# Feed-forward products in another order: sums of weights by accumulating DMA, left forms made at their first use, pool roles exchanged, and other prices in the planner

## The chip, the cores and the metric

The kernel runs on one core of a Trainium2 chip. A core has a matrix engine (TensorE, PE in the profile), a vector engine (VectorE, DVE), an activation engine (ScalarE, ACT), a general engine (GpSimd, POOL), a sequencer that mostly starts DMAs (SyncE, SP), and 16 DMA engines that move data between HBM and the on-chip memory SBUF. Matmul results go to PSUM, which has eight banks of 128 x 512 fp32. Each engine runs its instructions in program order; semaphores tie the engines together. The metric is the device time of one execution, in microseconds; lower is better.

## What is computed

A model of four layers on 512 tokens of width 1024, all in fp32. Each layer is a mixer (another one in each layer: RWKV-7, sliding-window attention, a spatial gating unit, gated linear attention) and a SwiGLU feed-forward network (FFN) of hidden width 2816:

```python
def swiglu(x, w_in, w_out):
    gate, up = jnp.split(x @ w_in, 2, axis=-1)
    return (jax.nn.silu(gate) * up) @ w_out
...
    for i in range(DEPTH):
        t, j = i % N_MIXERS, i // N_MIXERS
        hn = rmsnorm(h, norm_mix[i])
...
        h = h + m
        h = h + swiglu(rmsnorm(h, norm_ffn[i]), ffn_w_in[i], ffn_w_out[i])
    return rmsnorm(h, norm_final)
```

The change touches the FFN and what feeds it. The mixers compute the same as before, in code that isn't touched.

## The kernel before

**A product in three matmuls.** Every fp32 operand is split into a high half in a reduced fp32 format and a low half, the rest: ACT copies the high half (`whi`), DVE subtracts to get the low half (`wlo`; both in `split`). `mm3` then adds up high x high, high x low and low x high in the same PSUM bank.

**Seven products instead of eight.** Each FFN matrix is cut into 2 x 2 quarters, and a 2 x 2 block product is done with seven quarter products m1 to m7 (Strassen's way, in a form whose sums chain). `seven` (L764) writes them down: it loads one quarter of weights at a time into `wraw` tiles (`load`, two DMAs of 512 KB on SP's queue for a quarter of 512 x 512), forms sums of weights in place, and multiplies by "left forms", that is quarters of the activations and their sums: x11, x12 and x22 are quarters; s5 = x22 - x21, and s6, s7, s3 follow from it (`combine`, L649). A sum of weights is made either by an accumulating DMA that POOL issues, which adds another quarter from HBM into a `wraw` tile (`add`), or by a DVE addition of two tiles. With p, s and r for three pairs of PSUM banks, and with the weight quarters 0 to 3 of which a, e, b and c are loaded from 0, 1, 2 and 3, the order is:

```
m1: p  = x11 * a            (a = W0)
m2: s  = x12 * e            (e = W1)
m5: r  = s5  * b            (b = W2, + W0 by accumulating DMA)
m6: p += s6  * b            (b += c, on DVE)
m3: r += s3  * c            (c = W3)
m7: p += s7  * c            (c += W2, by accumulating DMA)
m4: p += x22 * b            (b += W1, by accumulating DMA)
```

A product of a full quarter is 24 matmuls: four blocks of the inner dimension, two output banks, three matmuls each. The generator yields after each product, and its caller empties the banks.

**Where it runs.** `ffn` (L722) goes through three parts of the hidden width. Each part has two `hidden` blocks (L828, gate and up projections, SiLU, product, transposition) and one `out_fast` (L751, down projection, added into the residual `h`). Four of the six hidden blocks have quarters 512 columns wide (weights `ffn_w_a`), two 384 (`ffn_w_b`); the output weights are `ffn_o_a` and `ffn_o_b`. The first two products of the next hidden block are written ahead of each output block. In `hidden`, ACT copies m1, m5, m6 and m7 out of PSUM (`copy`) into tiles that wait for their partners; `give` multiplies gate and up and transposes them into the quarters of the output product. In the last output block of a layer, `finish` (L593) follows when a quarter of `h` is complete: it takes the squares for the norm, transposes the quarter and scales it into quarters of the next product.

**Left forms.** Those of the hidden blocks are made once for an FFN, in `quarter` (L640), called by `finish` as soon as the data is there. They stay for all six blocks. Those of an output product are made when `seven` asks for them, through `left_of` (L747). `operand` (L709) hands the left forms to the FFN.

**Pools.** `wraw` has 8 buffers (`wr`), `whi` and `wlo` four each; PSUM tiles (`ps`) 8; general 128 x 512 tiles come from `slot()` (L509, 45 buffers, "slot") or from `more()` (L513, 15 buffers, "left").

**What sets the order on the engines.** The code above only records operations. Class `Program` (L190) then plans all of them: at each step `run` takes the operation that could start first by its prices, within a window of 700 operations, and writes it to its engine. `price` (L262) holds the estimated nanoseconds of an operation; `record` (L225) notes the size of a DMA in `columns`, which `run` turns into a transfer time. Where the planner foresees that PE would idle, `keep_warm` (L391) inserts fill products (L453, 128 x 128 by the identity, result unused) to keep PE's clock up. So whatever is recorded is issued from line 233, and names of tiles, not lines, tell the work apart. Nothing of the plan is fixed on the chip but the order within an engine.

## Time and profile before

| | |
|---|---|
| time, median of 3 runs | 2758.0 us (2755.4 to 2764.08) |
| the profiled execution | 2758.16 us, of which the span of the profile is 2756.5 us |
| mean granted PE clock in it | 0.981 of full speed |
| read from HBM, written | 324.90 MB, 2.10 MB |
| the four FFNs in the span | 556 to 937, 1108 to 1488, 1768 to 2131, 2373 to 2745 us |

A row of a view by groups gives the engine, the operation, output tile <- input tiles, shapes and count, then busy time and mean nanoseconds of one, then the idle time just before. A row of a timeline gives start, length, engine and what ran; brackets hold idle time before it and what ended that. "[0.2 <-DVE wlo L233]" says that the engine sat idle for 0.2 us until a `wlo` was written by DVE. Fills count as busy PE, so a high busy share of PE alone does not say that its time is used.

### The profile page before, as it was taken

How to read it: one execution, taken by the hardware profiler on the slowest of the kernel's cores; microseconds unless marked ns; L12 is line 12 of the kernel's file. 1: busy time of each engine (PE TensorE's matmuls, PEld its weight loads, DVE VectorE, ACT ScalarE, POOL GpSimd, SP SyncE). 2: the span in 40 equal slices, each digit the busy share in tenths (PEclk: the TensorE clock that was granted, in tenths of full speed). 3: DMA queues.
4: the chain of work that ended last, by engine and by line, in shares of the span. 5: the costliest groups of instructions: out<-in, count | busy, mean ns of one | idle time of the engine just before them, and what ended most of it. 6: DMA issues, size and time to landing. Idle time of an engine off the chain costs nothing.

```text
span 2756.5 us, 35561 instructions
## 1 busy us (share of the span) xinstructions
PE 2604.9 (95%) x13368; PEld 2144.3 (78%) x13368; DVE 1900.8 (69%) x2888; ACT 1381.9 (50%) x2304; POOL 405.6 (15%) x420
## 2 busy tenths in 40 slices
PE   8999889999999999999999999998999999999997
PEld 7676678887778766977887888896877768887786
DVE  8687786667678775776777555566777644676767
ACT  4545443365556455655564333464645523564554
POOL 1023343211111232111112000011110000011110
PEclk9999999999999999999999999999999999999999
DMA  3210001356677332566774222286676222476773
GB/s 128 77 50 14 5 21 49 109 121 165 173 170 192 88 102 52 129 158 178 173 214 134 96 92 79 68 206 158 168 177 158 94 69 71 94 175 160 182 174 89
DMA packets 116780, 331.68 MB, mean 120 GB/s; under 512 B 12272, under 2 KB 19824, under 8 KB 116608
## 3 DMA queue, kind: packets, MB, share of 16 engines
q1 hardware_dynamic: 85504, 225.59, 24.5%
q0 software_dynamic: 31104, 103.82, 21.1%
q8 instruction: 105, 1.72, 0.3%
q14 instruction: 67, 0.55, 0.1%
HBM read 324.90 MB, written 2.10 MB: 119 GB/s over the span
## 4 chain that ended last, share of the span: by engine, by line
PE 67%; DVE 11%; issue 9%; DMA 6%; ACT 4%; POOL 2%; POOLq 0%; ACTq 0%; SPq 0%; DVEq 0%
PE ps L233 66%; DVE slot L233 3%; DMA wraw<-ffn_w_a 3%; DVE wlo L233 3%; DMA wraw<-ffn_w_b 2%; ACT whi L233 2%; DVE et L233 1%; POOL wraw L233 1%; ACT slot L233 1%; DMA wraw<-ffn_o_a 1%; DVE left L233 1%; PE ps L453 1%; DVE h L233 1%; DVE mx L233 0%; DVE st L233 0%
## 5 line engine op out<-in xcount | busy, mean ns | idle before, releaser
L233 PE MATMUL ps<-whi,slot 128*128 128x512 f32 (+1 forms) x5072 | 1564.1, 386 | 37.9 <-ACT whi L233 28.0
L233 PEld LDWEIGHTS ps<-whi,slot 128*128 128x128 f32 x5072 | 952.4, 190 | 206.0 <-ACT whi L233 33.9
L233 DVE TENSOR_TENSOR wlo<-wraw,whi 128x1024 fp32r<-128x1024 f32 (+2 forms) x628 | 721.6, 1156 | 531.1 <-ACT whi L233 529.2
L233 PE MATMUL ps<-wlo,slot 128*128 128x512 f32 (+1 forms) x2536 | 980.6, 387 | 24.0 <-DVE wlo L233 23.8
L233 ACT CAST whi<-wraw 128x1024 fp32r<-128x1024 f32 (+2 forms) x632 | 626.4, 993 | 694.5 <-PE ps L233 530.1
L233 PEld LDWEIGHTS ps<-wlo,slot 128*128 128x128 f32 x2536 | 482.1, 190 | 111.4 <-DVE wlo L233 31.4
L233 PE MATMUL ps<-slot,whi 128*128 128x512 f32 (+2 forms) x864 | 275.4, 396 | 2.0 <-DVE slot L233 1.3
L233 DVE TENSOR_TENSOR slot<-slot 128x512 fp32r<-128x512 f32 (+6 forms) x369 | 235.2, 660 | 33.9 <-ACT slot L233 26.6
L233 PEld LDWEIGHTS ps<-slot,whi 128*128 128x128 f32 (+2 forms) x864 | 156.9, 184 | 47.7 <-issue 7.1
L233 ACT CAST slot<-slot 128x512 fp32r<-128x512 f32 (+1 forms) x240 | 137.0, 604 | 86.0 <-DVE slot L233 57.1
L233 PE MATMUL ps<-slot,wlo 128*128 128x512 f32 (+2 forms) x432 | 169.7, 393 | 0.0
L233 POOL DMA_DIRECT2D wraw<-ffn_w_a x96 | 82.9, 863 | 569.7 <-DVE wlo L233 424.4
L233 POOL DMA_DIRECT2D wraw<-ffn_w_b x48 | 41.6, 873 | 790.7 <-DMA wraw<-ffn_w_b 498.3
L233 ACT COPY left<-ps 128x512 f32<-128x512 f32 (+1 forms) x196 | 108.3, 556 | 76.0 <-PE ps L233 75.8
L233 DVE TENSOR_TENSOR h<-h,ps 128x512 f32<-128x512 f32 x168 | 113.2, 683 | 24.6 <-PE ps L233 22.7
L233 ACT COPY slot<-ps 128x512 f32<-128x512 f32 (+2 forms) x137 | 71.4, 565 | 87.7 <-PE ps L233 87.0
L453 PE MATMUL ps<-ident 128*128 128x128 f32 x714 | 113.5, 300 | 1.6 <-POOL ident L233 1.4
L453 PEld LDWEIGHTS ps<-ident 128*128 128x128 f32 x714 | 104.1, 205 | 10.3 <-POOL ident L233 1.4
L233 PEld LDWEIGHTS ps<-slot,wlo 128*128 128x128 f32 (+2 forms) x432 | 79.6, 184 | 20.7 <-issue 2.5
L233 POOL DMA_DIRECT2D wraw<-ffn_o_a x48 | 41.4, 862 | 276.4 <-DVE wlo L233 113.9
L233 DVE TENSOR_TENSOR wraw<-wraw 128x1024 f32<-128x1024 f32 (+1 forms) x72 | 81.1, 1132 | 1.1
L233 PE MATMUL ps<-ident,left 128*128 128x128 f32 x352 | 58.2, 287 | 20.8 <-DVE left L233 20.7
(259 smaller groups left out, 2548.6 us busy)
## 6 DMA issues: line engine op xcount, KB each, us to landing
wraw<-ffn_w_a SPq DMA_DIRECT2D x128, 512.0 KB, 4.7
wraw<-ffn_w_a POOLq DMA_DIRECT2D x96, 512.0 KB, 6.0
wraw<-ffn_o_a SPq DMA_DIRECT2D x64, 512.0 KB, 4.8
wraw<-ffn_w_b SPq DMA_DIRECT2D x64, 384.0 KB, 3.6
wraw<-ffn_o_a POOLq DMA_DIRECT2D x48, 512.0 KB, 6.7
wraw<-ffn_w_b POOLq DMA_DIRECT2D x48, 384.0 KB, 6.0
wraw<-ffn_o_b SPq DMA_DIRECT2D x16, 512.0 KB, 4.4
wraw<-sg_w_v SPq DMA_DIRECT2D x16, 512.0 KB, 4.3
```

What stands on the lines that cost most here:

```text
L233: op = self.add(eng.name, lambda: getattr(eng.target, what)(*map(real, args), **{k: real(a) for k, a in kw.items()}), *self.price(eng.name ...
L453: self.nc.tensor.target.matmul(self.ps.tile_pool.tile([P, S], F32, name="ps")[:, :P], self.ident.real(), self.ident.real(), start=True, st ...
```

## The change

It does five things in the FFN code and the planner.

1. *Order and banks.* The order becomes m1, m2, m5, m3, m6, m7, m4. m3 has a pair of banks of its own (t) and is added to m5's result when it is evacuated, not in PSUM. In the hidden blocks ACT copies m1 and m5 alone; DVE adds m3, m6 and m7 from PSUM into m5's and m3's tiles. In the output blocks m5 is subtracted from two quarters of `h`, so that `finish` for that quarter follows m6.
2. *Sums of weights.* b += c on DVE becomes an accumulating DMA of W3 into b. All four sums of a run of seven products are now accumulating DMAs.
3. *Left forms.* `quarter` is gone; `operand` returns a function that makes a left form when `seven` first asks for it and keeps it. The request for s3 forms s6 in the tile of s and s3 from it in x12's tile; s6 and s7 follow at their own requests.
4. *Pools.* Quarters, s and the transposed hidden tiles come from `more()`; the tiles that hold evacuated products come from `slot()`.
5. *Prices.* A matmul with reduced-format operands costs n x 0.4167 + 13.5 ns in the planner (before + 2.5), and an accumulating DMA counts 1.85 times its bytes.

```diff
         if what == "dma_start":
-            op.columns = 4.0 * math.prod(views[0].shape)
+            op.columns = 4.0 * math.prod(views[0].shape) * (1.85 if "accum_op" in kw else 1.0)
         if what == "activation":
...
             if args[2].dtype == F32R:
-                return max(n * 0.4167 + 2.5, m * 0.83), 200.0
+                return max(n * 0.4167 + 13.5, m * 0.83), 200.0
             return max(n * 1.667 + 5.0, m * 1.667, 340.0 if n < 16 and m == P else 0.0), 200.0
...
     def more(self):
+        if self.left is None:
+            return self.slot()
         return self.left.tile([P, S], F32, name="left")
...
             if self.kind == 'fast':
-                x = self.slot()
+                x = self.more()
                 self.xq.setdefault((nh, half), []).append(x)
...
                 nc.vector.scalar_tensor_tensor(xl[:, t], src, self.g(k), xh[:, t], op0=ALU.mult, op1=ALU.subtract)
-        if self.kind == 'fast':
-            self.quarter(self.xq, self.nf, (nh, half), keep=True)
...
-    def quarter(self, q, out, key, keep):
-        if key in self.LEFT:
-            out[self.LEFT[key]] = self.parts(q[key])
-        if len(q) == 4 and all(len(v) == len(q[0, 0]) for v in q.values()):
-            for n in ('s5', 's6', 's7', 's3'):
-                out[n] = self.parts(self.combine(q, n))
     def combine(self, q, name):
         nc = self.nc
         x11, x12, x21, x22 = q[0, 0], q[1, 0], q[0, 1], q[1, 1]
         if name == 's5':
-            q['s'] = [self.slot()[:, :t.shape[-1]] for t in x21]
+            q['s'] = [self.more()[:, :t.shape[-1]] for t in x21]
         for u in range(len(x11)):
             if name == 's5':
                 nc.vector.tensor_sub(q['s'][u], x22[u], x21[u])
-            elif name == 's6':
+            elif name == 's3':
                 nc.vector.scalar_tensor_tensor(q['s'][u], q['s'][u], -1.0, x11[u], op0=ALU.mult, op1=ALU.subtract)
-            elif name == 's3':
-                nc.vector.scalar_tensor_tensor(q['s'][u], q['s'][u], -1.0, x12[u], op0=ALU.mult, op1=ALU.subtract)
-            else:
+                nc.vector.scalar_tensor_tensor(x12[u], q['s'][u], -1.0, x12[u], op0=ALU.mult, op1=ALU.subtract)
+            elif name == 's7':
                 nc.vector.tensor_sub(x21[u], x11[u], x21[u])
-        return x21 if name == 's7' else q['s']
+        return {'s7': x21, 's3': x12}.get(name, q['s'])
...
     def operand(self):
-        self.op = self.nf if self.nf else self.nx
-        return self.op
+        self.op = self.nx
+        if not self.xq:
+            return self.nx
+        q, made = self.xq, {}
+        def x(key):
+            if key not in made:
+                made[key] = self.left_of(q, key)
+            return made[key]
+        return x
...
         nc = self.nc
-        where = {'m1': [(0, 0, 1)], 'm2': [(0, 0, 1)], 'm5': [(1, 1, -1)], 'm6': [(0, 1, -1)], 'm3': [(0, 1, -1)],
+        where = {'m1': [(0, 0, 1)], 'm2': [(0, 0, 1)], 'm5': [(1, 1, -1), (0, 1, -1)], 'm3': [(0, 1, -1)], 'm6': [(0, 1, -1)],
                  'm7': [(1, 1, -1)], 'm4': [(1, 0, 1)]}
         for name, ps in self.seven(w, S, x, nsub):
             for half, nh, sign in where[name]:
                 for b in range(2):
                     c = self.h[half * 2 + b][:, nh * S:(nh + 1) * S]
                     (nc.vector.tensor_add if sign > 0 else nc.vector.tensor_sub)(c, c, ps[b])
-                if last and name in ('m2', 'm3', 'm7', 'm4'):
+                if last and name in ('m2', 'm6', 'm7', 'm4'):
                     self.finish(half, nh)
...
         c = load(3)
-        for t, o in zip(b, c):
-            nc.vector.tensor_add(t, t, o)
+        add(b, 3)
+        t = banks()
+        mm('s3', t, c, True, True)
+        yield 'm3', t
+        add(c, 2)
         mm('s6', p, b, False, True)
         yield 'm6', p
-        mm('s3', r, c, False, True)
-        yield 'm3', r
-        add(c, 2)
         mm('s7', p, c, False, True)
...
         def copy(ps):
-            e = [self.more()[:, :W] for _ in range(2)]
+            e = [self.slot()[:, :W] for _ in range(2)]
             for b in range(2):
...
                         nc.tensor.transpose(ps[:, (j * 2 + b) * P:(j * 2 + b + 1) * P], up[b][:, (j0 + j) * P:(j0 + j + 1) * P], self.ident)
-                t = self.slot()[:, :n * 256]
+                t = self.more()[:, :n * 256]
                 nc.scalar.copy(t, ps[:, :n * 256])
                 gs.setdefault((kh, half), []).append(t)
-        for name, ps in self.seven(w, W, lambda key: x[key]):
-            if name in ('m1', 'm5', 'm6', 'm7'):
+        for name, ps in self.seven(w, W, x):
+            if name in ('m1', 'm5'):
                 got[name] = copy(ps)
...
             elif name == 'm3':
-                up = got['m6']
+                got[name] = [self.slot()[:, :W] for _ in range(2)]
                 for b in range(2):
-                    nc.vector.tensor_add(up[b], ps[b], up[b])
-                give(up, 0)
-            elif name == 'm4':
-                gate[1] = [self.more()[:, :W] for _ in range(2)]
+                    nc.vector.tensor_add(got['m3'][b], ps[b], got['m5'][b])
+            elif name == 'm6':
+                for b in range(2):
+                    nc.vector.tensor_add(got['m3'][b], ps[b], got['m3'][b])
+                give(got['m3'], 0)
+            elif name == 'm7':
+                for b in range(2):
+                    nc.vector.tensor_add(got['m5'][b], ps[b], got['m5'][b])
+            else:
+                gate[1] = [self.slot()[:, :W] for _ in range(2)]
                 for b in range(2):
                     nc.scalar.activation(gate[1][b], ps[b], AF.Silu, scale=col[:, b + 2:b + 3])
-            if name == 'm7':
-                up = got['m7']
-                for b in range(2):
-                    nc.vector.tensor_add(up[b], up[b], got['m5'][b])
-            elif name == 'm4':
-                give(got['m7'], 1)
+                give(got['m5'], 1)
             yield
```

**How the order moves.** Counted over the program, PE's fills go from 357 to 160 matmuls: 145 stand ahead of the first FFN both before and now, behind that 212 before and 15 now. POOL's accumulating DMAs go from 216 to 288. DVE loses 72 additions of weight tiles, has 24 more additions into `h` and 48 more evacuations of hidden products; ACT has 96 copies fewer.

The first place is DVE's row at the start of FFN 1, up to the low weight half (`wlo`, 128x768) with which PE can begin m5. `slot<-slot` and `left<-left` are left forms and their low halves, `rs_t` and `rcol` the tiny steps of the norm, `left<-ps,left` the evacuation of m2. Before (one further row, `slot<-slot 128x512 x6`, with the first s5 subtractions, stands directly ahead of the piece):

```order
L233 SCALAR_TENSOR_TENSOR slot<-slot 128x512
L233 TENSOR_TENSOR slot<-slot 128x512
L233 SCALAR_TENSOR_TENSOR slot<-slot 128x512
L233 TENSOR_TENSOR slot<-slot 128x512 x5
L233 SCALAR_TENSOR_TENSOR slot<-slot 128x512 x2
L233 TENSOR_TENSOR rs_t<-rcol 128x4
L233 TENSOR_TENSOR left<-ps,left 128x384
L233 TENSOR_TENSOR slot<-slot 128x512 x2
L233 SCALAR_TENSOR_TENSOR rs_t<-ms,rs_t 128x4
L233 TENSOR_TENSOR left<-ps,left 128x384
L233 SCALAR_TENSOR_TENSOR rcol<-rs_t,rcol 128x4
L233 TENSOR_TENSOR wlo<-wraw,whi 128x768
```

Now, in the same place (ahead of the piece stand the two s5 subtractions, `left<-left`, with one tiny row between them):

```order
L233 SCALAR_TENSOR_TENSOR rcol<-rs_t,rcol 128x4
L233 TENSOR_TENSOR slot<-left,slot 128x512
L233 TENSOR_TENSOR rs_t<-rcol 128x4
L233 TENSOR_TENSOR slot<-left,slot 128x512
L233 SCALAR_TENSOR_TENSOR rs_t<-ms,rs_t 128x4
L233 TENSOR_TENSOR slot<-left,slot 128x512
L233 SCALAR_TENSOR_TENSOR rcol<-rs_t,rcol 128x4
L233 SCALAR_TENSOR_TENSOR left<-left 128x512
L233 TENSOR_TENSOR rs_t<-rcol 128x4
L233 TENSOR_TENSOR slot<-left,slot 128x512
L233 SCALAR_TENSOR_TENSOR rs_t<-ms,rs_t 128x4
L233 TENSOR_TENSOR wlo<-wraw,whi 128x768
```

From the first s5 subtraction to that half there were 18 operations of 128x512; there are seven now, with seven tiny ones between them. The evacuation of m2 moved behind the half.

The second place is PE at the same time, at the end of m2 and the start of m5. Before (`ps<-ident` are fills):

```order
L233 MATMUL ps<-whi,slot 128x384 x2
L233 MATMUL ps<-wlo,slot 128x384
L233 MATMUL ps<-whi,slot 128x384 x3
L453 MATMUL ps<-ident 128x128 x19
L233 MATMUL ps<-wlo,slot 128x384
L233 MATMUL ps<-whi,slot 128x384 x2
```

Now, with the numbers of the tiles, where ps_10020 is a bank of m2 and ps_10064 one of m5:

```order
L233 MATMUL ps_10020<-whi_9914,slot_9988 128x384
L233 MATMUL ps_10020<-wlo_9932,slot_9988 128x384
L233 MATMUL ps_10020<-whi_9914,slot_10004 128x384
L233 MATMUL ps_10064<-whi_10024,slot_10000 128x384
L233 MATMUL ps_10064<-wlo_10041,slot_10000 128x384
L233 MATMUL ps_10064<-whi_10024,slot_10014 128x384
```

The 19 fills between the two products are gone; m5 follows m2 directly.

The third place is POOL's queue at the first `ffn_o_a` output product of FFN 0. All rows are accumulating DMAs; a tile that returns in a later row is added to a second time. Before, 7013 and 7042 are the two tiles of b, 7058 and 7097 those of c, 7119 and 7146 those of b in the next hidden block:

```order
L233 DMA wraw_7013<-ffn_o_a 128x1024
L233 DMA wraw_7042<-ffn_o_a 128x1024
L233 DMA wraw_7119<-ffn_w_a 128x1024
L233 DMA wraw_7146<-ffn_w_a 128x1024
L233 DMA wraw_7013<-ffn_o_a 128x1024
L233 DMA wraw_7042<-ffn_o_a 128x1024
L233 DMA wraw_7058<-ffn_o_a 128x1024
L233 DMA wraw_7097<-ffn_o_a 128x1024
```

Now 6960 and 6978 are b, 6996 and 7035 are c, 7073 and 7103 the next block's b:

```order
L233 DMA wraw_6960<-ffn_o_a 128x1024
L233 DMA wraw_6978<-ffn_o_a 128x1024
L233 DMA wraw_7073<-ffn_w_a 128x1024
L233 DMA wraw_7103<-ffn_w_a 128x1024
L233 DMA wraw_6960<-ffn_o_a 128x1024
L233 DMA wraw_6978<-ffn_o_a 128x1024
L233 DMA wraw_6996<-ffn_o_a 128x1024
L233 DMA wraw_7035<-ffn_o_a 128x1024
L233 DMA wraw_6960<-ffn_o_a 128x1024
L233 DMA wraw_6978<-ffn_o_a 128x1024
```

b is added to three times where it was added to twice, and the second sum of c stands between b's second and third.

More of the change, by code (lines that the diff above doesn't have):

```diff
@@ L458, in __init__ @@
         self.kind = "plain"
-        self.nx = self.op = None
+        self.nx = self.op = self.left = None
+        self.xq = {}
     def pool(self, name, bufs, es=None, **kw):
@@ L590, in begin @@
         self.nx = [None] * KT
-        self.xq, self.nf = {}, {}
+        self.xq = {}
     def finish(self, half, nh):
```

## The prediction

> **What bounds the kernel now.** I read the shares of the engines first, then the time by stage, then what TensorE (PE) waited for, and last single stretches.
>
> ```profile
> span 2756.5 us, 35561 instructions
> PE 2604.9 (95%) x13368; PEld 2144.3 (78%) x13368; DVE 1900.8 (69%) x2888; ACT 1381.9 (50%) x2304; POOL 405.6 (15%) x420
> ```
>
> PE is the bound, but not all of it is work. The next view gives the busy time of each engine in the four FFNs (us from the span's start, length, PE, weight loads, VectorE (DVE), ScalarE (ACT), GpSimd (POOL), granted clock, busy share of the 16 DMA engines, GB/s). The row under them, of L453 alone, is that of the fill products, which compute nothing and keep the clock up where the planner foresees idle time.
>
> ```profile
> 556.00:937.00 381.00, 357.92 (x1699) 303.43 (x1698) 287.54 (x377) 214.92 (x317) 56.24 (x62) 0.97 0.65 162
> 1108.00:1488.00 380.00, 362.38 (x1753) 308.60 (x1750) 286.30 (x371) 215.74 (x320) 57.66 (x62) 0.98 0.69 173
> 1768.00:2131.00 363.00, 342.05 (x1643) 289.98 (x1642) 269.03 (x347) 204.80 (x297) 46.27 (x55) 0.99 0.67 163
> 2373.00:2745.00 372.00, 350.54 (x1665) 297.75 (x1664) 271.96 (x353) 201.67 (x290) 44.92 (x52) 0.98 0.62 150
> 556.00:2745.00 2189.00, 62.80 (x424) 61.69 (x424) 0.99 0.53 136
> ```
>
> The FFNs take 381 + 380 + 363 + 372 = 1496 us, and from 556 us on 62.8 us of PE's busy time are fills. What PE sat idle for, over the whole span (sum in us, times, longest):
>
> ```profile
> PE ps L233 <- ACT whi L233: 28.0, 21, 3.3
> PE ps L233 <- DVE wlo L233: 23.8, 25, 3.4
> PE ps L233 <- DVE left L233: 20.7, 14, 4.7
> ...
> PE ps L233 <- DVE et L233: 9.6, 7, 5.1
> ...
> PE ps L233 <- ACT left L233: 7.0, 4, 2.9
> ```
>
> "whi", "wlo" and "left" are weight halves and evacuated products, nearly all of the FFN. So what the FFNs can give is 28.0 + 23.8 + 20.7 + 7.0 = 79.5 us of idle and 62.8 us of fills: **142.3 us**. A matmul that is not held up costs what the next rows show: three in 0.68 us.
>
> ```profile
> 640.16 0.39 PE L233 MATMUL ps<-wlo,slot 128*128 128x512 f32 x1
> 640.39 0.61 PE L233 MATMUL ps<-whi,slot 128*128 128x512 f32 x2
> 640.84 0.39 PE L233 MATMUL ps<-wlo,slot 128*128 128x512 f32 x1
> ```
>
> That is 0.227 us each, and a product of 24 such matmuls takes 5.44 us.
>
> The Trainium skill (Trainium Kernel Development and Optimization, Performance Expectations) calls matmul busy time a bad metric for the distance to the roofline, since matmuls are pipelined, and would have weight loads read instead. The trace agrees: PE 95%, weight loads 78%. By the 95% alone the rival "nothing to win" below would stand higher than I put it.
>
> **First term: the start of each FFN.** PE and then DVE at the start of FFN 1:
>
> ```profile
> 1117.44 0.68 PE L233 MATMUL ps<-whi,slot 128*128 128x384 f32 x3
> 1117.96 5.30 PE L453 MATMUL ps<-ident 128*128 128x128 f32 x38
> 1125.86 0.67 PE L233 MATMUL ps<-wlo,slot 128*128 128x384 f32 x1 [2.60 <-DVE wlo L233]
> 1126.33 0.84 PE L233 MATMUL ps<-whi,slot 128*128 128x384 f32 x2
> ...
> 1129.46 0.34 PE L233 MATMUL ps<-wlo,slot 128*128 128x384 f32 x1
> ```
>
> ```profile
> 1112.50 3.82 DVE L233 TENSOR_TENSOR slot<-slot 128x512 f32<-128x512 f32 x6 [0.17 <-ACT slot L233]
> ...
> 1124.86 0.95 DVE L233 TENSOR_TENSOR wlo<-wraw,whi 128x768 fp32r<-128x768 f32 x1
> ```
>
> PE has finished m1 and m2 at 1117.96 and gets the low weight half of m5 at 1125.86: 7.9 us lost, then matmuls at half pace until 1129.46 (3.1 us, so 1.5 us more). DVE was at work all the time, on left forms that later products need: 18 operations of 128x512 stand between the first s5 subtraction and that half. Changed, 7 stand there, and 7 tiny ones. At 3.82 / 6 = 0.61 us the first come to 4.3 us, the tiny ones (128x4) I put at 0.6 us together, an estimate: the half is begun at 1117.4 instead of 1124.86 and is there at 1118.4. What becomes late next is m2, since the low halves of x12 are now made behind the s5 subtractions: I leave 1.6 us lost. Gain 7.9 - 1.6 + 1.5 = 7.8 us, four times: **31 us** (0 to 4 x 9.4 = 38).
>
> The Trainium skill (TensorE: Matmul & The Clock Gate, Part 1) has the clock fall to half after an idle window of about 3.4 us. The half pace above agrees. By that rule a bare wait of that length, which the fills no longer break, would cost another 1.7 us; were all four starts to keep one, the sum would be 7 us smaller.
>
> **Second term: sums that land late.** The chain of waits (start, length):
>
> ```profile
> 689.71 9.52 DMA wraw<-ffn_w_a
> ...
> 699.33 1.05 ACT whi L233
> ...
> 700.41 1.23 DVE wlo L233
> 701.64 1.87 DVE left L233 x3
> ...
> 703.64 29.98 PE ps L233 x127
> ```
>
> This is the sum of W22 and W12 for m7. It can only start when m3 has split W22, and m7 follows m3 at once. It lands at 699.23, and PE goes on at 703.64, about 4 us late. In the new order m6 stands between m3 and m7, and m3 between m5 and m6: 5.44 us more for each sum, so that even this slow one would be in time by about 1.4 us. I count the "left" row, 20.7 us, and half of the "whi" row, 14.0 us, as this kind, and 85% of it as won: **30 us** (0 to 34.7).
>
> **Third term: the rest.** Of 142.3 us, 4 x 7.9 = 31.6 are starts, 34.7 late sums and 7.0 the "ACT left" row. 69.0 us remain. At the four starts the fills come to about 5.3 us each (above), so 62.8 - 4 x 5.3 = 41.6 us of these 69 are fills elsewhere, most of them where weight halves and the sum b + c queue up on DVE, as here in FFN 0:
>
> ```profile
> 797.70 4.62 DVE L233 TENSOR_TENSOR wlo<-wraw,whi 128x1024 fp32r<-128x1024 f32 x4
> 802.35 1.23 DVE L233 TENSOR_TENSOR wraw<-wraw 128x1024 f32<-128x1024 f32 x1
> ```
>
> The change takes the last row, and its kind, from DVE. What it takes and gives by groups:
>
> ```profile
> L233 DVE TENSOR_TENSOR wraw<-wraw 128x1024 f32<-128x1024 f32 (+1 forms) x72 | 81.1, 1132 | 1.1
> L233 DVE TENSOR_TENSOR h<-h,ps 128x512 f32<-128x512 f32 x168 | 113.2, 683 | 24.6 <-PE ps L233 22.7
> L233 DVE TENSOR_TENSOR left<-ps,left 128x512 f32<-128x512 f32 x64 | 41.7, 683 | 0.2
> L233 ACT COPY left<-ps 128x512 f32<-128x512 f32 (+1 forms) x196 | 108.3, 556 | 76.0 <-PE ps L233 75.8
> ```
>
> DVE loses the 72 sums (81.1 us) and gains 24 additions into h (24 x 0.683 = 16 us) and two evacuations in each of 24 hidden blocks (48 x 0.683 = 33 us): 32 us less. ACT loses 4 copies in each of these (96 x 0.556 = 53 us), which is worth nothing by itself at 50% busy. The planner now leaves 15 of the 212 fills from the first FFN on (two records in the trace for each), so by its prices these gaps close. For a 512-column matmul that price is now 0.2269 us, before 0.2159, and the rows above gave 0.227. But DVE stays full in the output products. I take 60% of 69: **41 us** (0 to 69).
>
> **What it adds.** (a) m6, m7 and m4 now add into the same two banks without another product between, and in the hidden blocks DVE, not ACT, empties them after m6 and m7. Before, only m7 to m4 did so, in 36 runs of seven products (six hidden blocks and three output blocks in each of four layers), and it cost the 7.0 us of the "ACT left" row, 0.2 us a time. 36 more such places at 0.2 us: **-8 us**. At the high end each of 72 waits behind one weight half (1.23 us above), 89 us; I stay near the row. (b) POOL issues 72 more accumulating DMAs at 82.9 / 96 = 0.86 us, 62 us on an engine that is 15% busy; in its queue each stands behind a wait for a DVE half. They lengthen the DMA work:
>
> ```profile
> L233 POOL DMA_DIRECT2D wraw<-ffn_w_a x96 | 82.9, 863 | 569.7 <-DVE wlo L233 424.4
> ...
> q1 hardware_dynamic: 85504, 225.59, 24.5%
> q0 software_dynamic: 31104, 103.82, 21.1%
> ...
> wraw<-ffn_w_a POOLq DMA_DIRECT2D x96, 512.0 KB, 6.0
> ...
> wraw<-ffn_o_a POOLq DMA_DIRECT2D x48, 512.0 KB, 6.7
> ```
>
> All 216 sums are the software queue: 0.211 x 2756.5 = 582 us, so a third more is 194 us. The FFNs now hold 381 x 0.65 + 380 x 0.69 + 363 x 0.67 + 372 x 0.62 = 984 us of DMA work, then 1178. Hidden behind PE, it costs nothing; what it costs if the cover goes is the third rival. (c) The new prices also reorder the mixers. The first, where chains and not PE set the pace ("et" above is one), keeps its fills; I put it at 0, within the 9.6 us of that row either way.
>
> **Sum.** 31 + 30 + 41 - 8 = 94 us off the profiled span: 2662.5, and 2664 us with the 1.7 us that the execution (2758.16) takes around it. That execution is the median of the runs shown (2758.0) within 0.2 us.
>
> **Rivals.** *All of it goes* (0.15): 142.3 us and the four half-paced stretches (4 x 1.5 = 6 us) vanish. For it: only 15 fills are left. Against: waits that the planner did not foresee hold no fills, as the longest of the "left" row, 4.7 us of bare idle, shows. 2758.2 - 142.3 - 6 = **2610 us**.
>
> *The queue fills up* (0.20): the extra sums make all of them land later, so that the second term is lost and half of the third: 31 + 20 - 8 = 43, 2715 us. For it: a landing of 9.52 us beside a median of 6.0. Against: at a third more, 8 us, most are still in time.
>
> *The DMA engines become the bound* (0.08), the case on the other side. In the fullest longer stretch I found they were busy 0.78 of the time:
>
> ```profile
> 639.00:654.00 15.00, 15.00 (x68) 12.39 (x67) 12.21 (x19) 9.51 (x15) 1.72 (x2) 1.00 0.78 192
> ```
>
> If they cannot be held fuller over a whole FFN, 1178 / 0.78 = 1510 us against 1496: 14 us slower, 2772 us, and at 0.72 already 2898. It decides where the FFNs need more than 1178 / 1496 = 0.79; my forecast (1402 us) needs 0.84. Against: for some us, where the sums run, they were full already:
>
> ```profile
> 686.00:694.00 8.00, 8.00 (x37) 6.64 (x36) 2.67 (x3) 3.76 (x5) 1.73 (x2) 1.00 1.02 190
> ```
>
> *Nothing to win* (0.07): DVE at 69% only moves the waits from one product to the next, 2758 us.
>
> **Numbers.** The forecast has 0.50. The range takes in all-goes and the filled queue: 2605 to 2735 us, 0.85 of the cases. A measurement of this kernel can tell about 0.3% from no change; faster by more 0.85, within it 0.07, slower by more 0.08.
>
> **What would show it.** Right: no fill between m2 and m5 and under 2 us lost there; the "left" row under 5 us; fills from the first FFN on under 6 us; FFNs of about 345 to 355 us at a DMA share above 0.8. Wrong: sums that land after 9 us in the median (the queue), long idle for "slot" written by DVE between m6, m7 and m4 (emptying), or PE idle for "whi" as before.

## The result and the profile after

The changed kernel takes 2629.4 us (median of 4 runs, 2621.82 to 2641.05), the kernel before 2756.7 us (4 runs, 2751.23 to 2764.08): a ratio of **0.954**, 95% interval 0.9497 to 0.9584. The forecast was 2664, the range 2605 to 2735. The profiled execution of the changed kernel is the longest of its four, 2641.05 us, with a span of 2639.3.

The head of the page and two queues of it:

```profile
span 2639.3 us, 34990 instructions
PE 2554.7 (97%) x12974; PEld 2083.4 (79%) x12974; DVE 1853.8 (70%) x2888; ACT 1331.6 (50%) x2208; POOL 466.0 (18%) x492
...
q0 software_dynamic: 41472, 138.43, 29.1%
q1 hardware_dynamic: 85504, 225.59, 25.3%
```

The sums' queue went from 0.211 x 2756.5 = 582 us of DMA work to 0.291 x 2639.3 = 768; the prediction added 194 and got 776. POOL went from 15% to 18%. The view by stage, the four FFNs (columns as in the prediction):

```profile
579.00:919.00 340.00, 335.39 (x1596) 281.32 (x1594) 275.11 (x374) 199.64 (x288) 70.37 (x79) 1.00 0.86 206
1092.00:1433.00 341.00, 335.78 (x1603) 282.29 (x1601) 266.34 (x355) 198.62 (x286) 70.35 (x78) 1.00 0.88 212
1720.00:2059.00 339.00, 334.17 (x1593) 280.87 (x1591) 264.76 (x359) 198.03 (x287) 61.23 (x73) 1.00 0.86 206
2292.00:2628.00 336.00, 331.86 (x1576) 279.81 (x1575) 262.21 (x356) 190.46 (x272) 59.81 (x70) 1.00 0.83 193
```

340 + 341 + 339 + 336 = 1356 us, where they took 1496: 140 us less. The granted clock in them was 0.97 to 0.99 and is 1.00 now; the DMA share was 0.62 to 0.69 and is 0.83 to 0.88. The fills alone from FFN 0 on, and what PE sat idle for over the whole span (sum, times, longest):

```profile
579.00:2639.00 2060.00, 5.26 (x30) 5.13 (x30) 1.00 0.65 163
```

```profile
PE ps L233 <- DVE slot L233: 15.5, 29, 1.5
PE ps L233 <- DVE et L233: 9.9, 6, 3.5
PE ps L233 <- DVE h L233: 9.3, 8, 3.7
...
PE ps L233 <- DVE wlo L233: 3.9, 7, 1.2
```

62.8 us of fills became 5.26. The sums of PE's busy time in the four stages, 1412.9 us before and 1337.2 now, split the 140 us. Idle time of PE fell from 83.1 to 18.8 us, by 64.3; the fills fell by 57.5. The other 18 us are PE's own matmuls: the same work took 1350.1 us and takes 1331.9, with the clock at 1.00 in all four stages. Of the rows that carried the prediction, "whi" (28.0), "left" by DVE (20.7) and "left" by ACT (7.0) are gone, and "wlo" fell from 23.8 to 3.9. What is new in the FFNs is "slot" written by DVE: evacuated products, of which 10.0 us lie there (the row was at 9.9 us before, nearly all of it in the mixers).

But the span shrank by only 2756.5 - 2639.3 = 117 us, not 140. FFN 0 starts at 579.0 us, where it started at 555.3: **the first mixer, which computes what it did before, took 23.7 us longer** in this execution. Two questions follow: which of the five parts bring the 140 us, and whether the change causes the 24.

### The profile page after: what moved, and what is told of

It reads as the page before. It is cut to its first block, busy times and chain, and to the rows that moved or that the text cites. A ratio compares the mean times of both kernels' runs of the same rounds, so it can differ in the third digit from the quotient of the medians.

```text
span 2639.3 us, 34990 instructions
## 1 busy us (share of the span) xinstructions
PE 2554.7 (97%) x12974; PEld 2083.4 (79%) x12974; DVE 1853.8 (70%) x2888; ACT 1331.6 (50%) x2208; POOL 466.0 (18%) x492
## 3 DMA queue, kind: packets, MB, share of 16 engines
q0 software_dynamic: 41472, 138.43, 29.1%
q1 hardware_dynamic: 85504, 225.59, 25.3%
## 4 chain that ended last, share of the span: by engine, by line
PE 47%; DMA 5%; issue 5%; DVE 5%; ACT 2%; POOL 0%; SPq 0%; ACTq 0%; POOLq 0%; DVEq 0%
PE ps L233 47%; DMA wraw<-ffn_o_a 2%; DMA wraw<-ffn_w_b 2%; DVE slot L233 2%; DVE wlo L233 1%; ACT whi L233 1%; DVE left L233 1%; DMA wraw<-ffn_w_a 1%; ACT slot L233 1%; POOL wraw L233 0%; DVE h L233 0%; DVE mx L233 0%; DMA wraw<-ffn_o_b 0%; DMA slot<-sg_b_s 0%; DMA slot<-slot 0%
## 5 line engine op out<-in xcount | busy, mean ns | idle before, releaser
L233 PE MATMUL ps<-whi,slot 128*128 128x512 f32 (+1 forms) x5072 | 1548.3, 383 | 14.1 <-DVE slot L233 10.0
L233 ACT CAST whi<-wraw 128x1024 fp32r<-128x1024 f32 (+3 forms) x632 | 626.6, 995 | 695.5 <-PE ps L233 528.5
L233 POOL DMA_DIRECT2D wraw<-ffn_w_a x128 | 109.5, 857 | 502.7 <-DVE wlo L233 363.0
L233 DVE TENSOR_TENSOR slot<-ps,slot 128x512 f32<-128x512 f32 (+2 forms) x287 | 153.3, 566 | 60.4 <-PE ps L233 45.7
L233 DVE TENSOR_TENSOR slot<-left,slot 128x512 fp32r<-128x512 f32 (+1 forms) x214 | 138.9, 666 | 34.9 <-ACT slot L233 29.1
L233 ACT CAST slot<-left 128x512 fp32r<-128x512 f32 (+1 forms) x214 | 124.1, 606 | 31.8 <-PE ps L233 24.7
L233 PEld LDWEIGHTS ps<-ident,slot 128*128 128x128 f32 x580 | 68.3, 142 | 34.5 <-issue 9.5
L233 PE MATMUL ps<-ident,slot 128*128 128x128 f32 x580 | 89.6, 277 | 3.3 <-POOL slot L233 2.6
L233 ACT COPY left<-ps 128x512 f32<-128x512 f32 x100 | 50.6, 556 | 63.7 <-PE ps L233 63.7
L233 DVE TENSOR_TENSOR slot<-slot 128x512 fp32r<-128x512 f32 (+9 forms) x93 | 61.5, 666 | 18.5 <-ACT slot L233 17.1
```

Of the source, the lines that this page charges most:

```text
L233: op = self.add(eng.name, lambda: getattr(eng.target, what)(*map(real, args), **{k: real(a) for k, a in kw.items()}), *self.price(eng.name ...
```

## The experiments

All times below come from two readings: the ratio to the kernel before on the same chip, and the profile, split at the first 384-column matmul of FFN 0. What lies ahead of it is called the first mixer, the rest of the span "from FFN 0 on". Planned fills are those that the planner put in from FFN 0 on. Each profile is one execution. The two of the changed kernel differ by 0.9 us from FFN 0 on, but by 14.2 us in the first mixer.

| kernel | ratio, 95% interval | first mixer, us | from FFN 0 on, us | planned fills |
|---|---|---|---|---|
| before | 1 | 555.3 | 2201.2 | 212 |
| the changed kernel | 0.954 (0.9497 to 0.9584) | 579.0 | 2060.3 | 15 |
| the changed kernel again (a1) | 0.950 (0.948 to 0.952) | 564.8 | 2059.4 | 15 |
| without the new prices (e2) | 0.9587 (0.9549 to 0.9626) | 550.8 | 2087.9 | 46 |
| b + c on DVE (e3) | 0.9577 (0.9544 to 0.9609) | 566.2 | 2087.3 | 57 |
| forms made at once (e4) | 0.9634 (0.9604 to 0.9663) | 569.6 | 2097.0 | 85 |
| old written order (e5) | 0.9612 (0.9581 to 0.9643) | 570.0 | 2087.8 | 39 |
| old pool roles (e6) | 0.9571 (0.9556 to 0.9586) | 566.5 | 2077.8 | 27 |
| before + new prices (e1) | 0.982 (0.9801 to 0.984) | 575.7 | 2144.9 | 180 |
| before + price of the sums (e10) | 0.9835 (0.9814 to 0.9856) | 558.7 | 2152.3 | 243 |
| before + new order (e7) | 0.9758 (0.9727 to 0.9788) | 556.9 | 2135.0 | 180 |
| before + forms at first use (e12) | 0.9917 (0.9893 to 0.994) | 560.4 | 2180.6 | 204 |
| changed, old matmul price in the first mixer (e9) | 0.9452 (0.9432 to 0.9472) | 556.8 | 2058.6 | 13 |
| changed, one quarter loaded twice (e11) | 0.9569 (0.9537 to 0.9602) | 566.4 | 2070.1 | 20 |

The sets of runs were made on different chips, and the changed kernel itself is at 0.954 in one and at 0.950 in another. So small differences are read from the two columns of time, or within one set.

### Each part taken out of the changed kernel

**The prices (e2).** Both back to the old ones:

```diff
-                return max(n * 0.4167 + 13.5, m * 0.83), 200.0
+                return max(n * 0.4167 + 2.5, m * 0.83), 200.0
...
-            op.columns = 4.0 * math.prod(views[0].shape) * (1.85 if "accum_op" in kw else 1.0)
+            op.columns = 4.0 * math.prod(views[0].shape)
```

> The changed kernel planned with the old prices (matmul + 2.5 ns, accumulating DMAs at their bytes); the program is the same, the order isn't: 46 fills from the first FFN on where the changed kernel has 15. Theory A (the gain is the work that left DVE and the sums that land in time; prices matter little): the four FFNs take 1356 + 5 to 10 = 1361 to 1366 us, the median is within 10 us of the changed kernel's 2629. Rival B (the prices close the gaps): the FFNs lose 30 us or more, median above 2659. On the first mixer, which took 579 us in the changed kernel's profile and 555 before: if the order made by the new prices costs that, it is back at about 555 here; if its clock varies from run to run, it may come out anywhere between.

From FFN 0 on it loses 27.6 us, between the two expectations and far nearer to B. "whi" is back in PE's idle view, five waits of up to 3.3 us:

```profile
PE ps L233 <- DVE slot L233: 22.9, 24, 2.7
PE ps L233 <- ACT whi L233: 12.7, 5, 3.3
```

The first mixer is at 550.8 us, 28 us less than in the changed kernel's first profile and 14 us less than in its second.

**The sum b + c (e3).**

```diff
-        add(b, 3)
+        for u, o in zip(b, c):
+            nc.vector.tensor_add(u, u, o)
         t = banks()
```

> The changed kernel with the sum b + c made by a DVE addition again (72 of 1.13 us) and not by an accumulating DMA; 216 sums by DMA as before, 57 planned fills. Theory A (that sum in DVE's queue was a large part of the third term): the FFNs lose 30 to 41 us, 1386 to 1397, median about 2660 to 2670, with PE idle for weight halves again. Rival B (the other parts keep DVE off the path): less than 10 us, median below 2639; DVE busier by 81 us and nothing later.

27.0 us more from FFN 0 on: just under A's 30, well above B. It shows first in the fills, 17.74 us where the changed kernel has 5.26. Over the span, idle for "slot" written by DVE is at 23.2 us (15.5 in the changed kernel) and idle for "wlo" at 7.6 (3.9), so the waits for weight halves that A named are a small part.

**The forms (e4).** The removed `quarter` is put back into `finish`, with the sums in the order s5, s3, s6, s7:

```diff
+        if self.kind == 'fast':
+            if (nh, half) in self.LEFT:
+                self.nf[self.LEFT[nh, half]] = self.parts(self.xq[nh, half])
+            if len(self.xq) == 4 and all(len(v) == 2 for v in self.xq.values()):
+                for n in ('s5', 's3', 's6', 's7'):
+                    self.nf[n] = self.parts(self.combine(self.xq, n))
...
-            if key not in made:
-                made[key] = self.left_of(q, key)
-            return made[key]
+            return nf[key]
```

> The changed kernel with all seven left forms of an FFN made as soon as the norm has given the quarters, as before, not at their first use; 85 planned fills. Theory A (the starts were 31 us of the gain): each FFN starts with some 8 us of PE lost between m2 and m5, FFNs 1356 + 31 = 1387, median about 2660. Rival B (the starts come free by themselves because DVE has less else to do): under 10 us, median below 2640.

36.7 us more, and the start of FFN 1 looks as it did before the change. PE between m2 and m5:

```profile
1101.88 0.68 PE L233 MATMUL ps<-whi,slot 128*128 128x384 f32 x3
1102.40 4.98 PE L453 MATMUL ps<-ident 128*128 128x128 f32 x36
1110.04 0.66 PE L233 MATMUL ps<-wlo,slot 128*128 128x384 f32 x1 [2.66 <-DVE wlo L233]
```

7.64 us lost, as against 7.9 in the kernel before. In the changed kernel DVE, at the same place, needs this long from the first s5 subtraction to m5's low half:

```profile
1094.79 0.69 DVE L233 TENSOR_TENSOR left<-left 128x512 f32<-128x512 f32 x1
...
1099.62 0.95 DVE L233 TENSOR_TENSOR wlo<-wraw,whi 128x768 fp32r<-128x768 f32 x1
```

4.83 us; the prediction had 4.9. PE was still at m2 then, and nothing was lost between m2 and m5.

**The written order (e5).** `seven`, `hidden`, `out_fast` and `combine` of before, with the sum by DMA and the new pool roles:

```diff
+        add(b, 3)
         mm('s6', p, b, False, True)
         yield 'm6', p
-        t = banks()
-        mm('s3', t, c, True, True)
-        yield 'm3', t
+        mm('s3', r, c, False, True)
+        yield 'm3', r
+        add(c, 2)
```

> The changed kernel with the old way to write the products (m6 before m3, m3 added to m5's banks, ACT copies of m5, m6 and m7), all four sums still by DMA, lazy forms, new pools and prices; 39 planned fills. Theory A (the written order gives the sums their time): the late sums come back and the b + c sum is a late one too, FFNs 30 us or more longer, 1386 or above, median 2660 or above. Rival B (the planner moves m3 ahead of m6 by itself where the sum is not there, as its order for this kernel does in most places; the written order is worth little): within 10 us of 2629.

27.5 us more: nearer to A than to B. "whi" comes back:

```profile
PE ps L233 <- DVE slot L233: 13.2, 24, 1.4
PE ps L233 <- ACT whi L233: 13.2, 15, 2.5
```

**The pools (e6).** `more()` and `slot()` exchanged again in `hidden`, `combine` and `finish`.

> The changed kernel with the pool roles of before (quarters, sums and transposed hidden tiles from the 45, evacuated products from the 15); 27 planned fills. Theory A (the pools bind nothing; the other parts made the gain): FFNs within 8 us of 1356. Rival B (15 tiles are too few for evacuated products when two products more wait in them): PE idle for tiles written by DVE or ACT in the FFNs, FFNs 15 us or more longer.

17.5 us more: A falls, and the 15 us or more of B came. The wait for evacuated products grows and changes its name with the pool, and "whi" has some again:

```profile
PE ps L233 <- DVE left L233: 13.2, 19, 2.3
PE ps L233 <- DVE slot L233: 7.2, 10, 2.0
PE ps L233 <- ACT whi L233: 6.0, 6, 1.9
```

The five parts, each taken out alone, cost 27.6 + 27.0 + 36.7 + 27.5 + 17.5 = 136.3 us of the 140.9. That looks as if they simply added up. The next set shows that they don't.

### Each part alone, on the kernel before

**Both prices (e1)**, the diff of e2 the other way round.

> The kernel before with the two new prices alone; 180 planned fills from the first FFN on (212 before). Taking the prices out of the changed kernel cost its FFNs and later mixers 28 us together and gave 28 us back in the first mixer. Theory A (the prices only help where the other parts have left room): the FFNs gain 5 to 15 us of 1496, the first mixer loses about 15, median within 10 us of before. Rival B (the prices are worth some 28 us by themselves): FFNs 1470 or below, median 10 us or more below before.

B's bounds hold, but its 28 us are half of what came: 56.3 us less from FFN 0 on. The first mixer took 20.4 us more, where A had about 15. Two numbers in the planner, with nothing changed in the FFN's own code, bring 40% of what the whole change brings there.

**The price of the sums alone (e10).**

> The kernel before with the price of accumulating DMAs alone (1.85 times the bytes), matmuls at the old price; 243 planned fills from the first FFN on. Both new prices together took 56 us off the FFNs and later mixers and added 20 us to the first mixer. If the planner mainly had to know how late sums land: 35 us or more of the 56 come here, idle for left written by DVE falls to about 6 us. If it mainly had to know how long PE takes for its matmuls (so that DVE and ACT are not put behind a PE that is thought too fast): less than 15 us, or slower for its 31 more fills. The first mixer, whose plan holds no such sum, stays at 550 to 557 us either way.

48.9 us of the 56.3. The first mixer is at 558.7, 3.4 us above before and just outside the 550 to 557 that was expected, with PE's order there unchanged. So most of the gain is the price of the sums (the matmul price alone was not tried), and it comes with *more* planned fills, 243 for 212. PE's idle view of e10:

```profile
PE ps L233 <- DVE wlo L233: 21.9, 24, 3.5
PE ps L233 <- ACT whi L233: 19.4, 23, 2.1
...
PE ps L233 <- DVE left L233: 0.8, 1, 0.8
```

"left" went from 20.7 us in 14 waits to 0.8 in one. How that came about is seen at the place whose chain the prediction quoted, m7 in FFN 0. PE and then DVE there, in the kernel before:

```profile
699.64 0.40 PE L233 MATMUL ps<-whi,slot 128*128 128x512 f32 x1
703.64 0.66 PE L233 MATMUL ps<-ident,left 128*128 128x128 f32 x2 [3.61 <-DVE left L233]
```

```profile
696.62 1.23 DVE L233 TENSOR_TENSOR wlo<-wraw,whi 128x1024 fp32r<-128x1024 f32 x1 [4.96 <-ACT whi L233]
700.41 1.23 DVE L233 TENSOR_TENSOR wlo<-wraw,whi 128x1024 fp32r<-128x1024 f32 x1 [2.57 <-ACT whi L233]
701.55 1.28 DVE L233 TENSOR_TENSOR left<-ps,left 128x512 f32<-128x512 f32 x2
702.75 1.40 DVE L233 SCALAR_TENSOR_TENSOR left<-left,ncol 128x512 f32<-128x512 f32 x2
```

and in e10:

```profile
697.78 0.39 PE L233 MATMUL ps<-whi,slot 128*128 128x512 f32 x1
698.02 0.38 PE L233 MATMUL ps<-ident,left 128*128 128x128 f32 x2
```

```profile
694.54 1.23 DVE L233 TENSOR_TENSOR wlo<-wraw,whi 128x1024 fp32r<-128x1024 f32 x1 [1.02 <-ACT whi L233]
695.68 1.28 DVE L233 TENSOR_TENSOR left<-ps,left 128x512 f32<-128x512 f32 x2
696.88 1.41 DVE L233 SCALAR_TENSOR_TENSOR left<-left,ncol 128x512 f32<-128x512 f32 x2
698.75 1.23 DVE L233 TENSOR_TENSOR wlo<-wraw,whi 128x1024 fp32r<-128x1024 f32 x1 [0.46 <-ACT whi L233]
```

In both, the last `wlo` belongs to the second tile of the late sum for m7. Before, it stands ahead of the four `left` operations; two of them add m3 from PSUM to m6, the next two multiply the result, and PE transposes it (`ps<-ident,left`). m3 was ready at about 697, when PE went on to m7. DVE runs in order, so it stands still for 2.57 us until the sum has landed and ACT has made its `whi`. The `left` tiles wait with it, and so do the transposes in PE's queue among m7's matmuls: 3.61 us of idle PE. With the higher price of a sum the planner puts `left` first, and PE goes on without a wait. The sums of `ffn_w_a` land no sooner in e10 (6.2 us in the median, 6.0 before).

**The new order alone (e7)**: m3 with banks of its own ahead of m6, evacuated by DVE; the sum b + c stays on DVE.

> The kernel before with the new order and banks of the products alone (m3 with its own banks ahead of m6, DVE empties m3, m6 and m7), the sum b + c still on DVE, forms made at once, old pools and prices; 180 planned fills from the first FFN on. Taken out of the changed kernel, the order cost 27.5 us outside the first mixer. Theory A (the parts add up): some 27 us less than before in the FFNs, 2170 to 2180 us outside the first mixer (2201 before), median 20 to 32 us below before, idle for left written by DVE under 10 us. Theory D (the parts need each other: with all of DVE's work and forms made at once, an order with more work for DVE frees little): less than 12 us.

66.2 us less, more than twice A. PE's idle view of e7:

```profile
PE ps L233 <- DVE wlo L233: 21.0, 15, 2.9
PE ps L233 <- DVE h L233: 10.5, 11, 2.5
PE ps L233 <- DVE left L233: 10.4, 14, 2.8
...
PE ps L233 <- ACT whi L233: 2.2, 3, 1.2
```

Nearly all of "whi" is gone (28.0 to 2.2), not the half that the prediction put down to late sums, and the row of ACT's "left" (7.0) too. "left" by DVE is halved (20.7 to 10.4, where A had under 10), and the fills went from 62.80 to 52.40 us. The sums land later here than before, those of `ffn_w_a` after 7.0 us in the median (6.0), so an earlier landing is not what helps; it fits that PE has a product to do meanwhile.

Order and price work in part on the same rows. The price of the sums took 19.9 us of "left" by DVE, 8.6 of "whi" and all of ACT's "left"; the order took 10.3, 25.8 and 7.0. Alone, order and both prices bring 66.2 and 56.3 us, but either can be taken out of the changed kernel for some 27.5. The two together without the other parts were not tried, and neither were b + c by DMA alone or the new pools alone on the kernel before.

**The forms at first use alone (e12).**

> The kernel before with the left forms of the hidden blocks made at their first use and nothing else changed; 204 planned fills from the first FFN on. Taken out of the changed kernel, this cost 37 us outside the first mixer. Theory A (the first term of the prediction, 31 us, stands by itself): 25 to 37 us less in the FFNs, no fills between m2 and m5. Theory D (the parts need each other; what leaves the start comes back where DVE makes the forms later among weight halves and sums): less than 15 us.

20.6 us less, between A and D. The time that PE loses in the first 25 us of each FFN (every gap between two matmuls beyond their pace of 0.227 or 0.174 us) adds up to 39.2 us in the four FFNs before, 5.9 in the changed kernel and 12.9 in e12. Between m2 and m5 only FFN 0 keeps fills, three planned ones. With old prices and old order, PE waits for a `whi` some 13 us into the later FFNs instead (2.2 us lost in FFN 1, most of it under fills), and over the span that row rises from 28.0 to 32.7 us:

```profile
PE ps L233 <- ACT whi L233: 32.7, 31, 3.2
```

### The first mixer, and the DMA engines

**The old matmul price for the first mixer alone (e9)**, all else as in the changed kernel:

```diff
-                return max(n * 0.4167 + 13.5, m * 0.83), 200.0
+                return max(n * 0.4167 + (13.5 if self.later else 2.5), m * 0.83), 200.0
...
         nc, d = self.nc, self.d
+        nc.later = True
         col = self.rcol()
         neg = self.sm.tile([P, NB], F32, name="ncol")
```

> The changed kernel with the old matmul price for what is recorded before the first FFN, and the new prices behind it: PE's order in the first mixer is word for word that of before, 13 planned fills in the FFNs. Profiles so far give the first mixer 555 and 551 us where the old matmul price ordered it, 579, 566, 570 and 570 where the new one did. Theory A (the new price makes a slower order there, which works against the gain): the first mixer takes 550 to 556 us, FFNs stay at 1356 within 6, and the median is 12 to 22 us below the changed kernel's on the same chip. Rival C (the first mixer's time is set by how its clock happens to fall in a run, not by the order): 560 to 580 us in the profile, median within 6 us of the changed kernel's.

> The changed kernel again, unaltered, on the same chip as the others of this set, for comparison. Theory A: the first mixer 566 to 580 us, the four FFNs 1356 within 6 us, the median 0.954 of before. Rival C: the first mixer may come out at 555 us as well.

On one chip, e9 is at 0.9452 (0.9432 to 0.9472) and the changed kernel at 0.950 (0.948 to 0.952): 2614.0 and 2626.1 us, 12 us apart, with intervals that don't touch. **e9 is faster than both kernels.** Its first mixer, 556.8 us, is just above the 550 to 556 of A. From FFN 0 on the two are alike (2058.6 and 2059.4). Over all profiles, the first mixer took 550.8 to 560.4 us in the six whose order there comes from the old matmul price, and 564.8 to 579.0 in the eight with the new one. PE's instructions stand there in one order in all of the six, and in one other in all of the eight. C is right in part: the granted clock moves too. The first 550 us of e9, of the changed kernel and of the changed kernel again (a1), all engines:

```profile
0.00:550.00 550.00, 506.56 (x3411) 413.17 (x3412) 403.04 (x747) 246.44 (x475) 145.76 (x141) 0.96 0.18 56
```

```profile
0.00:550.00 550.00, 505.55 (x3260) 406.02 (x3261) 388.34 (x726) 238.63 (x457) 140.25 (x137) 0.92 0.14 45
```

```profile
0.00:550.00 550.00, 500.87 (x3367) 406.10 (x3368) 397.09 (x740) 243.38 (x464) 145.45 (x141) 0.96 0.16 52
```

a1 has 0.96 as e9 has and still takes 8 us more. So some 8 us are the order's, and the rest up to 24 us, in the execution that was profiled first, came with a lower clock. The clock over these 550 us was 0.95 to 0.98 in the six profiles with the old order and 0.92 to 0.96 in the eight with the new one. The new order may thus lower the clock too, but the two ranges overlap, and no run separates this.

**More DMA work (e11).** W1 of each run of seven products is loaded twice into the same tile:

```diff
         e = load(1)
+        for (k, n), raw in zip(us, e):
+            nc.sync.dma_start(raw, w[1][:, k * W:(k + n) * W])
```

> The changed kernel with one weight quarter of each run of seven products (W1) loaded twice into the same tile: a quarter more plain loads in the FFNs, 33.5 MB, about 99 us of DMA work at the rate of the other loads, on top of 1163; 20 planned fills. Theory A (the DMA work is hidden at a share of 0.86, and more of it can be): a share of about 0.93 and the FFNs within 10 us of 1356, median within 12 us of the changed kernel's 0.950 of before. Rival E (0.86 to 0.88 is all that the DMA engines can be filled to): FFNs of 1262 / 0.87 = 1450, some 90 us slower.

The FFNs by stage:

```profile
566.00:913.00 347.00, 336.97 (x1605) 282.50 (x1603) 275.75 (x375) 199.82 (x289) 70.38 (x79) 1.00 0.91 226
1086.00:1428.00 342.00, 334.96 (x1597) 281.68 (x1597) 265.99 (x353) 198.69 (x286) 69.48 (x78) 1.00 0.94 234
1716.00:2055.00 339.00, 334.83 (x1595) 281.36 (x1594) 264.92 (x358) 197.76 (x286) 61.05 (x73) 1.00 0.92 230
2288.00:2625.00 337.00, 332.55 (x1574) 279.61 (x1573) 262.35 (x356) 189.77 (x271) 59.68 (x70) 1.00 0.88 216
```

In the FFNs A holds, and E falls: a share of 0.94 over 342 us, and that FFN takes 1 us more. All of them together take 9 us more, 7 of it in FFN 0. The median misses A's bound: 2639.8 us is 19 us above 0.950 x 2758.9 = 2621.0. Against the other ratio of the changed kernel, 0.954, it is 8 us above; the changed kernel was not run in this set. The sums of `ffn_w_a` land later, after 8.4 us in the median where the changed kernel has 6.0, and most of that is hidden too.

## Why the prediction came out as it did

It had the direction, the place (the FFNs) and, in the range, the size. The forecast of 2664 us was 35 us too slow. From FFN 0 on the kernel gained 140.9 us where 94 were forecast, 47 more; the first mixer, forecast at 0, took 23.7 us of that back; and the profiled execution, with which the sum is compared, lies 12 us above the median of its runs. The two errors have opposite signs, so it is in part luck that the total lies well inside the range: at the 0.9452 of e9, without the loss in the first mixer, it would be 0.9452 x 2756.7 = 2605.6 us, at the range's lower end of 2605.

- **First term, the starts: right.** 31 us forecast; the starts lost 39.2 - 5.9 = 33 us less, and taking the part out cost 36.7. Between m2 and m5 one planned fill is left, 0.38 us in FFN 0, and none in the others. One slip in its working changed little: 3.82 / 6 is 0.64 us, not 0.61, so DVE's stretch comes to 5.1 us and not 4.9; it took 4.83. No start keeps a bare wait as long as the prediction weighed there: the longest gap in the first 25 us is 1.5 us.
- **Second term, sums that land late: right about the rows, too small.** 30 us forecast. "It can only start when m3 has split W22, and m7 follows m3 at once" is so, and with a product in between nearly all of the "whi" row went, not half. But the "left" row came from a wait in DVE's queue, ahead of work that was ready, and the order alone takes only half of it; the price of the sums alone takes nearly all. The order alone brings 66.2 us.
- **Third term, the rest: mis-sized.** 60% of 69 us was taken as won, because "DVE stays full in the output products". Nearly all of it went: fills are at 5.26 us, "wlo" at 3.9. This step also gave the new prices the smallest role, a line on how near they are to the rows; they bring 56.3 us alone. And it read the planner's fills as a measure ("15 of the 212"): e10 has 31 fills more than before and is 48.9 us faster.
- **Left out: PE's own matmuls.** The prediction counted 1.5 us of half pace at each of the four starts. The matmuls of the FFNs took 18 us less in all.
- **(a) Emptying the banks: about right.** 8 us were charged beside the 7.0 that was there (36 x 0.2 is 7.2). In the FFNs, the matmuls that read a high weight half now wait 10.0 us for "slot" and 3.9 for "h", 13.9 together.
- **(b) More DMA work: right.** Hidden, as forecast, with 1163 us in the FFNs (340 x 0.86 + 341 x 0.88 + 339 x 0.86 + 336 x 0.83) for 1178.
- **(c) The first mixer at 0: wrong.** It "keeps its fills", and it does, 145 of them; but its order changed with the matmul price. That cost some 8 us at the same clock and 12 us in the comparison of medians; in the profiled execution, with its lower clock, the first mixer was 24 us longer.

So the sum was 94 forecast, and 140.9 - 23.7 = 117.2 us measured in the profile. Of the rivals, *all of it goes* comes nearest for the FFNs: 148.3 us with the half-paced stretches, 140.9 measured from FFN 0 on. It is not what happened row by row: idle time and fills in the FFNs fell by 121.8 us, since new waits came, and the matmuls gave 18. *The queue fills up* did not come: sums of `ffn_w_a` land after 6.0 us in the median as before, those of `ffn_o_a` after 7.5 (6.7). *The DMA engines become the bound* would have begun at a share of 0.79; the FFNs ran at 0.83 to 0.88, and e11 at up to 0.94.

## What to carry to other kernels

When a planner orders the engines, a wrong price is a change to the kernel: look for an instruction that waits at the head of an in-order queue while ready work stands behind it, and ask which price put it there. Edits can look additive when each is taken out of the finished kernel, as here, and turn out to remove the same waits when each is tried alone; both tests are needed. A price that is right in one stage can give a slower order in another, so read every stage after such a change, the untouched ones too.

## What the runs showed that had not been expected

- An accumulating DMA cost 1.9 times a plain load per byte here: 138.43 MB in 768 us of DMA work, against 225.59 MB in 0.253 x 2639.3 = 668 us.
- The DMA engines held a share of 0.94 over a stretch of 342 us (e11), of which PE was busy 334.96 us at a clock of 1.00.
- From run to run the time moved with the mean granted clock: the four runs of the changed kernel took 2641.05, 2632.49, 2626.32 and 2621.82 us at 0.982, 0.985, 0.989 and 0.990. In the profiled one, the first 550 us ran at 0.92 and the FFNs at 1.00.
